# Splitting the second norm's operands group by group, with one head of ff1

## The chip, the cores and the metric

The kernel runs on one core of a Trainium2 chip. The metric is the device time of one execution in microseconds (us), as the median of several runs. The engines named here are TensorE (PE; its weight loads are shown as PEld), VectorE (DVE), ScalarE (ACT), GpSimd (POOL) and SyncE (SP); POOL and SP also issue DMAs, each in order from a queue of its own.

## The reference

One layer on 512 tokens of width 2048, all in float32:

```python
h = rmsnorm(x, g_mix)
z = h @ w_in                    # conv B, C, V | attention Q, K, V | forget logits | gates
conv_branch = (cb * causal_dwconv(cc * cv, conv_w)) @ w_conv_out
attn_branch = forgetting_attention(q, k, v, log_f) @ w_attn_out
merged = sigmoid(gate_c + ..) * conv_branch + sigmoid(gate_a + ..) * attn_branch
x = x + merged @ w_mix_out
h = rmsnorm(x, g_mlp)
u = square(relu(h @ w_ff1))     # 2048 -> 8192
x = x + u @ w_ff2               # 8192 -> 2048
out = rmsnorm(x, g_final)
```

## The kernel before

**Split operands.** Every matmul operand is split into a rounded high part and the rest: ACT copies it to a narrower float32 form (`th`, line 103), DVE subtracts that copy (`tl`, line 104). A product is then three matmuls: high by high, low by high, high by low. `th` and `tl` have two buffers each, so the next product's split runs beside the present one.

**Seven products for eight.** A `Group` (line 178) makes 512 columns of a product from four quarters X(i, j) of the weights, in Winograd's form: seven block products A11, A12, S1, S2, S3, S4, A22 of 48 matmuls each, instead of eight. DVE makes the sums of weight quarters (line 107) and puts the results together (line 110). The activations need the same seven combinations ("parts"), made and split beforehand. `head` runs A11 and A12, `tail`, `tail2` and `tail3` the other five in different orders; `head(True)` keeps its two quarters for the tail, `head()` lets them go, and the tail loads them again.

**Order of the stages.** Tile, the layer below, reorders instructions by its own estimate of when each is ready, engine by engine; what it leaves stands in order on each engine and queue. The stages that concern us follow one another so:

- `conv_out(c)` and `attn_out(c)`, c = 0 to 3: the two branches' projections, 512 columns each. `conv_out` multiplies its result by the convolution gate and, for c > 0, stores it in `held_d`; `bring(c)` loads it back into `merged`; `attn_out` adds the gated attention branch to it. `all_of(c)` makes and splits the seven parts of `merged[c]` into tiles `M` (placed by `M.place` in the buffers t0 to t6).
- Mixing groups g = 0 to 3 (`Mix`, line 1010): the product with `w_mix_out` and the residual sum. `turn` transposes each result with PE into `F`; `sums` makes the parts of the second norm's output from it. For g < 3 they are stored unsplit in `f_d` (`out`, line 1066).
- While group 3 and the first heads of ff1 run, `begin_part` loads each part from `f_d` into one of t0 to t6, and `split_part` splits it; group 3's own quarter is split straight into place.
- ff1: groups 0 to 15. Five `heads` of groups 0 to 4 run early, with `tail2` later; groups 5 to 15 run as head and `tail`. `put_u` squares the results, makes their parts for ff2 and stores them in `s_d`; `r` and `rh` have one buffer each. For the five early groups the squared first quarter goes through DRAM (`hu_d`).
- ff2: eight segments of two units each; `load_sums` loads the parts of a segment into t1 to t4.

**Starts.** The tiles `th` and `tl` are a little longer than their contents: a group of 256 columns starts `shift` elements into the tile. Groups have `SHIFT = 16` elements (64 bytes), mixing group g has `16 * g`: 0, 64, 128 and 192 bytes. In the mixing and value groups (`mm_rows`) this tile streams; in the others (`mm_cols`) it is the stationary operand. Some products start with one short extra matmul of 192 columns (`extra="first"`, `apart`), which changes no result.

Of the kernel before, what the change touches and what calls it, by code (L numbers as in the profile page):

```python
# [8 lines left out]
F32 = mybir.dt.float32  # L9
# [3 lines left out]
ALU = mybir.AluOpType  # L13
# [32 lines left out]
def tile_hybrid_block(ctx: ExitStack, tc, x, g_mix, w_in, b_f, b_gate, conv_w, w_conv_out,  # L46
# [33 lines left out]
    f_d = dram.tile([P, 7, KT // 2 - 2, HS], F32, name="f_d")  # L80
    hu_d = dram.tile([5, P, 2, HS], F32, name="hu_d")
# [20 lines left out]
    def split(src, hi, lo, one=1.0):  # L102
        nc.scalar.activation(out=hi, in_=src, func=AF.Copy, scale=one)  # L103
        nc.vector.tensor_tensor(out=lo, in0=src, in1=hi.bitcast(F32), op=ALU.subtract)  # L104

    def sub(out, a, b):
        nc.vector.tensor_tensor(out=out, in0=a, in1=b, op=ALU.subtract)  # L107
# [70 lines left out]
    class Group:  # L178
# [3 lines left out]
        def __init__(self, view, c1, c2, w, ST, mm, banks, put, scale=1.0, extra={}, after={}, shift=SHIFT):  # L182
            self.extra, self.after, self.shift = extra, after, shift
            self.view, self.cs, self.w, self.ST, self.mm, self.banks = view, (c1, c2), w, ST, mm, banks
            self.put, self.scale, self.at = put, scale, {}
            self.nq = view.shape[0] // (2 * P)
# [103 lines left out]

        def tail2(self):
# [3 lines left out]
            sub(X[0, 0], X[0, 1], X[0, 0])  # L295
            c = self.acc("c")
            self.run(c, "S1", X[0, 0], True)
            sub(X[0, 1], X[1, 1], X[0, 1])
# [553 lines left out]
    class Products:  # L852
# [5 lines left out]
        def tile(self, t, units):  # L858
            for e, u in enumerate(units):
                self.at[u] = t[:, e]  # L860
# [4 lines left out]
        def moving(self, n):  # L865
            return lambda q: tuple(self.at[n, q // 2][:, e, q % 2, :] for e in range(2))

        def quads(self, c, t):
# [3 lines left out]
            def put(n, src):  # L872
                split(src, self.at[n, c][:, 0], self.at[n, c][:, 1])
# [27 lines left out]
    def conv_out(c, banks):  # L901

        gates = {}
        for i, j in ((0, 0), (1, 1), (0, 1), (1, 0)):
            gates[i, j] = pc_.tile([P, 2, HS], F32, tag="hg", name="gates", bufs=4)
            k = 4 * c + 2 * j
            nc.gpsimd.dma_start(out=gates[i, j], in_=g_d[0, k:k + 2, :, i * HS:(i + 1) * HS].rearrange("k p s -> p k s"))
        if c == 0:
            place_merged(c)
# [22 lines left out]
    def place_merged(c):  # L932

        if c < 3:
# [36 lines left out]
    M.place(4, [(n, 0) for n in ("A11", "A12", "S1", "S3")])  # L971
    M.place(6, [("S2", 0), ("S4", 0), ("A22", 0), ("A22", 1)])
# [7 lines left out]
    M.place(1, [("S1", 1), ("S3", 1), ("S1", 2), ("S3", 2)])  # L980
    M.place(5, [("S2", 1), ("S4", 1), ("S2", 2), ("S4", 2)])
# [3 lines left out]
    M.tile(pm.tile([P, 1, 2, 2, HS], F32R, tag="m22", name="M"), [("A22", 2)])  # L985
# [13 lines left out]
    PARTS = ("A11", "A12", "A22", "S1", "S3", "S2", "S4")  # L999

    def begin_part(n, k):

        Q2[n] = pair(k, F32R, n).rearrange("p e (q s) -> p e q s", q=KT // 2)
        nc.gpsimd.dma_start(out=Q2[n][:, 1, :KT // 2 - 2].bitcast(F32), in_=f_d[:, PARTS.index(n)])

    def split_part(n):
        lo = Q2[n][:, 1, :KT // 2 - 2]
        split(lo.bitcast(F32), Q2[n][:, 0, :KT // 2 - 2], lo)

    class Mix:  # L1010


        def __init__(self, g):
            self.g, self.last = g, g == 3
            self.F = [pm.tile([P, 2, 2, HS], F32, tag=f"f{i}", name="f") for i in range(2)]
            self.x, self.missing = {}, []
# [19 lines left out]
        def turn(self, i, j, v):  # L1036
# [7 lines left out]
            if self.last and i == 0:  # L1044
                for par, n in enumerate(("A11", "A12")):
                    if n not in Q2:
                        self.missing.append((n, par, j))
                        continue
# [426 lines left out]
```

## Time and profile before

| | |
|---|---|
| Median of 3 runs | 2476.23 us (2475.4 to 2479.29) |
| Profiled execution, its own time | 2482.86 us |
| Its span | 2481.2 us, granted PE clock 0.991 |
| PE / weight load / DVE / ACT / POOL busy | 98% / 92% / 82% / 48% / 11% |
| HBM read, written | 385.47 MB, 107.48 MB |

The profile is one execution with every instruction's start and end. A row `L104 DVE TENSOR_TENSOR tl<-x,th ... x280 | 639.6, 2288 | 168.8` names line, engine, operation, what it writes and reads, how often, its total busy us, the mean ns of one, and the engine's idle time before these. In the order of time a row begins with start and duration in us; a bracket gives the idle time before it and what ended it. `A`, `S` and `M` are parts of activations, `x` and `y` weight quarters.

### The profile page before, as it was taken

To read this page: it belongs to the slowest core of one execution; us is meant where nothing else is said; L and a number is where in the kernel's file an instruction comes from. 1 tells how busy PE (TensorE), PEld (TensorE's weight loads), DVE (VectorE), ACT (ScalarE), POOL (GpSimd) and SP (SyncE) were. 2 spreads that over 40 slices of the span, in tenths; PEclk is the share of its full clock that TensorE was granted. 3 is DMA by queue.
4 is the path that set the end of the run, shared out by engine and by line. 5 is a ranking of instruction groups with operands and counts; after the bars stand their busy time and mean duration, and the time that the engine had idled before them with its cause. 6 is when DMAs were issued, how large, how long until landed. Compare 5 with 4: busy or idle time off the path is not lost. (4 is left out here: it accounts for less than half of the span.)

```text
span 2481.2 us, 41527 instructions
## 1 busy us (share of the span) xinstructions
PE 2425.0 (98%) x17799; PEld 2280.6 (92%) x17799; DVE 2044.8 (82%) x1711; ACT 1201.6 (48%) x1223; POOL 277.7 (11%) x443
## 2 busy tenths in 40 slices
PE   8999999999999999999898999999999999999998
PEld 8999899999999999899898899999997888888886
DVE  6987777688888778788887788988988888889898
ACT  6433443445545534355655556666665333333334
POOL 0100000111111111112100000000011000100000
PEclk9999999999999999999999999999999999999999
DMA  7564544464555755565856656466587566655763
GB/s 247 181 193 145 158 131 130 136 191 152 196 196 180 255 186 197 166 197 186 277 195 231 234 190 239 174 211 224 188 286 269 203 240 213 244 183 185 257 217 105
DMA packets 295788, 495.64 MB, mean 200 GB/s; under 512 B 11932, under 2 KB 208660, under 8 KB 295220
## 3 DMA queue, kind: packets, MB, share of 16 engines
q1 hardware_dynamic: 246432, 292.64, 37.3%
q0 software_dynamic: 48304, 199.25, 21.7%
q8 instruction: 139, 2.28, 0.4%
q10 hardware_dynamic: 868, 1.10, 0.1%
q14 instruction: 45, 0.37, 0.0%
HBM read 385.47 MB, written 107.48 MB: 199 GB/s over the span
## 5 line engine op out<-in xcount | busy, mean ns | idle before, releaser
L104 DVE TENSOR_TENSOR tl<-x,th 128x2048 fp32r<-128x2048 f32 (+1 forms) x280 | 639.6, 2288 | 168.8 <-ACT th L103 153.6
L103 ACT ACTIVATE th<-x 128x2048 fp32r<-128x2048 f32 (+1 forms) x280 | 536.6, 1917 | 476.2 <-DVE x L107 135.3
L107 DVE TENSOR_TENSOR x<-x,x 128x2048 f32<-128x2048 f32 (+1 forms) x160 | 366.1, 2288 | 32.5 <-DMA x<-in_w_in_dram 16.0
L103 ACT ACTIVATE th<-y 128x2048 fp32r<-128x2048 f32 (+1 forms) x109 | 184.8, 1700 | 270.3 <-PE a L167 138.9
L104 DVE TENSOR_TENSOR tl<-y,th 128x2048 fp32r<-128x2048 f32 (+1 forms) x109 | 219.0, 2014 | 25.7 <-ACT th L103 25.2
L147 PE MATMUL c<-S,th 128*128 128x256 f32 x912 | 212.1, 278 | 2.8 <-ACT o L212 2.8
L149 PE MATMUL c<-S,th 128*128 128x256 f32 x912 | 211.4, 277 | 0.0
L166 PE MATMUL a<-th,us 128*128 128x512 f32 x512 | 199.9, 390 | 2.0 <-ACT th L103 2.0
L167 PE MATMUL a<-th,us 128*128 128x512 f32 x512 | 200.0, 391 | 0.0
L147 PE MATMUL a<-S,th 128*128 128x256 f32 x720 | 169.6, 280 | 5.4 <-ACT th L103 5.4
L147 PEld LDWEIGHTS c<-S,th 128*128 128x128 f32 x912 | 171.4, 188 | 3.7 <-ACT o L212 3.2
L149 PEld LDWEIGHTS c<-S,th 128*128 128x128 f32 x912 | 171.4, 188 | 0.0
L149 PE MATMUL a<-S,th 128*128 128x256 f32 x720 | 168.0, 278 | 0.0
L147 PEld LDWEIGHTS a<-S,th 128*128 128x128 f32 x720 | 136.4, 189 | 6.0 <-ACT th L103 6.0
L147 PE MATMUL b<-A,th 128*128 128x256 f32 x544 | 130.2, 283 | 8.7 <-ACT th L103 8.7
L169 PE MATMUL a<-tl,us 128*128 128x512 f32 x512 | 137.3, 390 | 0.0
L149 PEld LDWEIGHTS a<-S,th 128*128 128x128 f32 x720 | 136.5, 190 | 0.0
L149 PE MATMUL b<-A,th 128*128 128x256 f32 x544 | 129.7, 282 | 0.0
L147 PE MATMUL a<-A,th 128*128 128x256 f32 x544 | 126.7, 278 | 0.0
L147 PE MATMUL d<-S,th 128*128 128x256 f32 x544 | 126.6, 278 | 0.0
L149 PE MATMUL a<-A,th 128*128 128x256 f32 x544 | 126.5, 278 | 0.0
L149 PE MATMUL d<-S,th 128*128 128x256 f32 x544 | 126.0, 277 | 0.0
(367 smaller groups left out, 6088.2 us busy)
## 6 DMA issues: line engine op xcount, KB each, us to landing
x<-in_w_in_dram SPq DMA_DIRECT2D x86, 1024.0 KB, 5.9
x<-in_w_ff_dram SPq DMA_DIRECT2D x74, 1024.0 KB, 8.0
y<-in_w_ff_dram SPq DMA_DIRECT2D x64, 1024.0 KB, 7.8
us<-s_d POOLq DMA_DIRECT2D x48, 1024.0 KB, 9.4
s_d<-rh POOLq DMA_DIRECT2D x32, 896.0 KB, 5.3
s_d<-r POOLq DMA_DIRECT2D x32, 896.0 KB, 8.2
x<-in_w_mix_out_dram SPq DMA_DIRECT2D x16, 1024.0 KB, 6.5
g_d<-o POOLq DMA_DIRECT2D x32, 256.0 KB, 2.8
```

Of the source, the lines that this page charges most:

```text
L103: nc.scalar.activation(out=hi, in_=src, func=AF.Copy, scale=one)
L104: nc.vector.tensor_tensor(out=lo, in0=src, in1=hi.bitcast(F32), op=ALU.subtract)
L107: nc.vector.tensor_tensor(out=out, in0=a, in1=b, op=ALU.subtract)
L147: nc.tensor.matmul(o, hi[:, q, js], Sh, start=first and q == 0 and j == 0, stop=False, skip_group_check=True)
L149: nc.tensor.matmul(o, hi[:, q, js], Sl, start=False, stop=False, skip_group_check=True)
L166: nc.tensor.matmul(o, Sh, hi[:, q, :], start=begin and q == 0, stop=False, skip_group_check=True)
L167: nc.tensor.matmul(o, Sl, hi[:, q, :], start=False, stop=False, skip_group_check=True)
L169: nc.tensor.matmul(o, Sh, lo[:, q, :], start=False, stop=q == nq - 1, skip_group_check=True)
```

## The change

- Each mixing group g < 3 splits its parts S1, S2, S3, S4 and A22 when it makes them, in a pair of `staged` buffers, and stores both halves in `h_d`. A11 and A12 still go unsplit to `f_d` and are split after loading. The five parts are handed out over the next group's products (`give`) instead of all at once.
- `begin_part` of the last group loads whole split parts; two parts come before ff1, more as buffers come free.
- ff1 has one head ahead: group 0 runs `head(True)` and `tail2`, groups 1 to 15 run like 5 to 15 before. `hu_d` and `fetch` go.
- `conv_out(1)`, `(2)` and `(3)` follow one another; the convolution gate of c > 0 is multiplied in `attn_out` from a tile `hg` of its own, and `bring` runs two column groups ahead.
- `M` holds parts by product rather than by column group, so that buffers come free product by product; the third A22 waits in `staged` and is copied.
- Some steps are kept in program order: behind the instruction traced before them on their engine.
- All mixing groups start at `shift=48` (192 bytes).
- Two of the first `load_sums` of ff2 are issued after A12 of the first unit.

The core of the diff:

```diff
-    f_d = dram.tile([P, 7, KT // 2 - 2, HS], F32, name="f_d")
-    hu_d = dram.tile([5, P, 2, HS], F32, name="hu_d")
+    f_d = dram.tile([P, 2, KT // 2 - 2, HS], F32, name="f_d")
+    h_d = dram.tile([P, 5, 2, KT // 2 - 2, HS], F32, name="h_d")
...
+    def split_in_order(*how):
+        for i in split(*how):
+            tc.keep_in_program_order(i)
...
+        def first_sum(self):
+            self.pinned = True
+            X = self.X
+            X[0, 1] = self.load(0, 1)
+            tc.keep_in_program_order(sub(X[0, 0], X[0, 1], X[0, 0]))
...
-            sub(X[0, 1], X[1, 1], X[0, 1])
+            third = sub(X[0, 1], X[1, 1], X[0, 1])
+            if self.pinned:
+                tc.keep_in_program_order(third)
...
     def conv_out(c, banks):
...
         def put(i, j, v):
             ts = slice(i * HS, (i + 1) * HS)
-            o = whole_of[c][:, i, :, j, :] if c == 0 else v
-            nc.vector.tensor_tensor(out=o, in0=v, in1=gates[i, j], op=ALU.mult)
-            if c > 0:
-                nc.gpsimd.dma_start(out=held_d[c, 2 * j:2 * j + 2, :, ts].rearrange("k p s -> p k s"), in_=o)
+            if c == 0:
+                nc.vector.tensor_tensor(out=whole_of[c][:, i, :, j, :], in0=v, in1=gates[i, j], op=ALU.mult)
+            else:
+                nc.gpsimd.dma_start(out=held_d[c, 2 * j:2 * j + 2, :, ts].rearrange("k p s -> p k s"), in_=v)
...
         def cons_at(j, ps):
+            if c > 0:
+                hg = otile([P, S], "hg")
+                nc.gpsimd.dma_start(out=hg, in_=g_d[0, 4 * c + j])
+                onto(c, j, hg, ALU.mult)
...
             if last and j == 2:
-                M.place(2, [(n, 3) for n in ("A11", "A12", "S1", "S3")])
-                M.place(3, [(n, 3) for n in ("S2", "S4", "A22")])
+                M.place(2, [(n, 3) for n in ("A11", "A12", "S1", "S2")])
+                M.place(3, [("S4", 3), ("S3", 3), ("A22", 3), ("A22", 2)])
+                for e in range(2):
+                    nc.gpsimd.dma_start(out=M.at["A22", 2][e].bitcast(F32), in_=m22[e].bitcast(F32))
...
     def all_of(c):
         for step in M.quads(c, merged[c]).values():
             step()
-        bring(c + 1)
+        if c < 2:
+            bring(c + 2)
...
     conv_out(0, lower)
     attn_out(0, upper)
     conv_out(1, lower)
-    attn_out(1, upper, between={0: lambda: all_of(0)})
-    conv_out(2, lower)
-    conv_out(3, upper)
-    M.place(0, [("A11", 1), ("A12", 1), ("A11", 2), ("A12", 2)])
...
+    conv_out(2, upper)
+    conv_out(3, lower)
+    M.place(0, [("A11", 0), ("A11", 1), ("A11", 2), ("A12", 0)])
...
+    m22 = M.at["A22", 2] = staged(), staged()
+    bring(1)
+    attn_out(1, upper, between={0: lambda: all_of(0)})
     attn_out(2, lower, between={0: lambda: all_of(1)})
     attn_out(3, upper, between={0: lambda: all_of(2)}, order=(0, 2, 1, 3), last=True)
...
     def begin_part(n, k):
         Q2[n] = pair(k, F32R, n).rearrange("p e (q s) -> p e q s", q=KT // 2)
-        nc.gpsimd.dma_start(out=Q2[n][:, 1, :KT // 2 - 2].bitcast(F32), in_=f_d[:, PARTS.index(n)])
+        if n in SPLIT:
+            nc.gpsimd.dma_start(out=Q2[n][:, :, :KT // 2 - 2].bitcast(F32), in_=h_d[:, SPLIT.index(n)])
+        else:
+            nc.gpsimd.dma_start(out=Q2[n][:, 1, :KT // 2 - 2].bitcast(F32), in_=f_d[:, int(n == "A12")])
...
             else:
-                nc.gpsimd.dma_start(out=f_d[:, PARTS.index(n), 2 * g:2 * g + 2], in_=src)
+                hi = staged()
+                split_in_order(src, hi, src)
+                for e, o in enumerate((hi.bitcast(F32), src)):
+                    nc.gpsimd.dma_start(out=h_d[:, SPLIT.index(n), e, 2 * g:2 * g + 2], in_=o)
...
             after.add("A11", before.sums)
+            for n, part in (("A12", "S1"), ("S1", "S3"), ("S2", "A22")):
+                after.add(n, lambda before=before, part=part: before.give(part))
...
             after.add("A12", lambda: begin_part("A11", 0))
-            after.add("S1", lambda: split_part("A11"))
-            after.add("S4", mix.fourth)
-            after.add("S3", lambda: begin_part("A12", 4), lambda: split_part("A12"), mix.supply)
-            after.add("A22", lambda: begin_part("S1", 1))
+            after.add("S2", lambda: begin_part("S1", 1), lambda: begin_part("S3", 2))
+            after.add("S4", mix.fourth, lambda: split_part("A11"))
+            after.add("S3", lambda: begin_part("S2", 5))
+            after.add("A22", lambda: begin_part("S4", 6), lambda: begin_part("A22", 3), lambda: split_part("A12"))
         group = Group(w_mix_out, g * S, g * S + HS, HS, M.moving, mm_rows, steady(g), mix.put, after=after,
-                      shift=16 * g)
+                      shift=48)
+        if g == 0:
+            after.add("A11", group.first_sum)
...
-    heads = [ff1(g, ((a,), (3,), (1,), (7,))) for g, a in enumerate((5, 0, 2, 4, 5))]
...
-    heads[3].tail2()
-    heads[4].tail2()
+    g0 = ff1(0, ((5,), (0,), (1,), (7,)))
+    g0.after = Steps(A11=[turn_waiting, mix.sums], A12=[lambda: mix.out("S1", mix.parts["S1"]),
+                                                        lambda: factors(common, turned)])
+    g0.head(True)
+    for n in SPLIT[1:]:
+        mix.out(n, mix.parts[n])
...
+    g0.tail2()
...
-    for g in range(AHEAD, DFF // S):
+    for g in range(1, DFF // S):
...
-    load_sums(0, (1, 2, 3), us0)
+    load_sums(0, (1,), us0)
...
+        if seg == 0 and cg == 0:
+            load_sums(0, (2, 3), us0)
```

More of the change, by code (lines that the diff above doesn't have):

```diff
@@ L865, in moving @@
         def moving(self, n):
[L866 removed]
+            return lambda q: tuple(e[:, q % 2, :] for e in self.at[n, q // 2])
         def quads(self, c, t):
@@ L1055, in turn @@
             if (i, j) == (0, 1) and not self.last:
-                for par, n in enumerate(("A11", "A12")):
-                    self.out(n, self.F[0][:, par])
-        def supply(self):
-            for n, par, j in self.missing:
-                split(self.F[0][:, par, j], *(Q2[n][:, e, 2 * self.g + j, :] for e in range(2)))
+                for par in range(2):
+                    nc.gpsimd.dma_start(out=f_d[:, par, 2 * g:2 * g + 2], in_=self.F[0][:, par])
         def fourth(self):
@@ L1079, in sums, with give @@
             sub(a12, a12, a11)
-            self.parts = {"S1": s1, "S3": a21, "S2": a11, "S4": a12, "A22": a22}
+            self.parts = {"S2": a11, "S4": a12, "S1": s1, "S3": a21, "A22": a22}
             if not self.last:
-                for n, src in self.parts.items():
-                    self.out(n, src)
+                self.give("S2", "S4")
+        def give(self, *names):
+            for n in names:
+                self.out(n, self.parts[n])
     waiting = []
@@ L1186, in put @@
             quarters[i, j] = v
-            if (i, j) == (0, 0) and g < AHEAD:
-                square(v, v)
-                nc.gpsimd.dma_start(out=hu_d[g], in_=v)
-            elif (i, j) == (0, 0):
+            if (i, j) == (0, 0):
                 later.append(hold)
```

80 lines of the change are left out of this document (28 added, 52 removed).

## The prediction, as made before the run

> **What bounds the kernel now.** I read the page first, then busy time by stretches, then the waits and the order of time inside the stretches that fell short. The page says that TensorE (PE) is the bound, and that at most 56 us of its span are idle (2481.2 less 2425.0):
>
> ```profile
> span 2481.2 us, 41527 instructions
> ...
> PE 2425.0 (98%) x17799; PEld 2280.6 (92%) x17799; DVE 2044.8 (82%) x1711; ACT 1201.6 (48%) x1223; POOL 277.7 (11%) x443
> ```
>
> A busy share hides slow matmuls, so I count matmuls per stretch. The columns are PE, weight load, DVE, ACT and POOL busy with counts, granted clock, DMA share, GB/s. In order: the last convolution group, mixing groups 0 to 3, the first head of ff1, its other heads, its tails, one steady ff1 group.
>
> ```profile
> 968.00:989.50 21.50, 20.34 (x172) 19.67 (x172) 18.97 (x23) 11.01 (x14) 4.37 (x6) 1.00 0.58 196
> 1033.60:1081.60 48.00, 44.15 (x344) 43.45 (x343) 40.09 (x40) 23.16 (x29) 3.63 (x5) 0.93 0.40 116
> 1081.60:1123.00 41.40, 41.40 (x354) 41.33 (x353) 32.86 (x25) 21.82 (x36) 9.71 (x15) 1.00 0.64 198
> 1123.00:1165.00 42.00, 41.89 (x356) 41.69 (x354) 33.36 (x25) 22.08 (x36) 9.69 (x15) 1.00 0.61 194
> 1165.00:1215.00 50.00, 43.21 (x355) 42.80 (x353) 39.65 (x33) 29.84 (x50) 13.15 (x21) 0.90 0.80 265
> 1215.00:1250.00 35.00, 35.00 (x302) 35.00 (x301) 31.59 (x30) 25.17 (x30) 5.49 (x8) 1.00 0.71 230
> 1250.00:1317.00 67.00, 65.83 (x579) 65.64 (x578) 53.83 (x37) 35.65 (x36) 3.80 (x7) 1.00 0.66 219
> 1317.00:1453.70 136.70, 119.75 (x963) 117.74 (x964) 109.40 (x86) 72.59 (x77) 9.66 (x18) 0.95 0.63 213
> 1492.00:1530.10 38.10, 38.10 (x338) 38.10 (x337) 33.76 (x27) 24.40 (x26) 2.13 (x4) 1.00 0.59 208
> ```
>
> The steady row gives 38.10/338 = 0.1127 us per matmul. Each stretch less its count at that pace is what it loses: 2.1, 9.2, 1.5, 1.9, 10.0, 1.0, 1.7 and 28.2 us. The start of ff2, with matmuls twice as wide, is set against its next 27 us (27/121 each):
>
> ```profile
> 1857.00:1884.00 27.00, 24.96 (x106) 19.92 (x105) 23.70 (x19) 15.87 (x17) 2.61 (x4) 0.94 0.85 304
> 1884.00:1911.00 27.00, 27.00 (x121) 22.37 (x120) 24.31 (x14) 13.60 (x12) 3.05 (x5) 1.00 0.69 252
> ```
>
> It loses 3.3. All stretches that the diff touches thus lose about 59 us; more than that the change cannot gain.
>
> **ff1 with one head.** Five heads run before any tail, and a head that does not keep its two quarters loads them again. The waits between 1317 and 1453.7 say what this costs (waiter, releaser, total us, times, longest):
>
> ```profile
> PE b L147 <- ACT th L103: 8.7, 2, 4.6
> ACT r L1154 <- DMA s_d<-r: 12.8, 2, 7.0
> ACT r L1149 <- DMA s_d<-r: 10.7, 2, 5.4
> DVE x L107 <- DMA x<-in_w_ff_dram: 4.8, 2, 3.5
> ```
>
> PE waits for ACT's copy `th`; ACT stands in order behind work on `r`, whose single buffer is still being stored; DVE waits for weights. In the DMA issues one sees the reload and the square's round trip:
>
> ```profile
> x<-in_w_ff_dram SPq DMA_DIRECT2D x74, 1024.0 KB, 8.0
> hu_d<-o POOLq DMA_DIRECT2D x5, 256.0 KB, 2.5
> f_d<-f POOLq DMA_DIRECT2D x18, 256.0 KB, 3.5
> S<-f_d POOLq DMA_DIRECT2D x4, 768.0 KB, 6.4
> ```
>
> Sixteen groups of four quarters are 64 loads; 74 means ten repeats, 10 MB. After the change groups 1 to 15 run the code that groups 5 to 15 run now, and that code loses nothing in the steady row. So 28.2 + 1.7 = **-29.9**; the least is about -20 if a third of it comes from being near the norm rather than from the heads.
>
> **The start of ff1.** Removed are the splits of S1, S3, S2, S4 and A22 read back raw; only their last quarter is split there. What remains hangs on the last mixing product: its sum on DVE, transposes, sums, split of S1. First and last step in order of time, and between them what DVE did of splits in that stretch:
>
> ```profile
> 1215.29 0.69 DVE L110 TENSOR_TENSOR o<-d,o 128x512 f32<-128x512 f32 x1 [2.12 <-PE d L169]
> L104 DVE TENSOR_TENSOR S<-S 128x1536 fp32r<-128x1536 f32 x2 | 3.5, 1755 | 0.3 <-ACT S L103 0.3
> L104 DVE TENSOR_TENSOR A<-A 128x1536 fp32r<-128x1536 f32 x1 | 1.8, 1753 | 0.0
> 1230.79 0.67 DVE L104 TENSOR_TENSOR S<-s,S 128x512 fp32r<-128x512 f32 x1
> ```
>
> Today the chain takes 1231.46 - 1215.29 = 16.2 us with three splits of 1.75 in it, and three heads cover it. One head covers 96 matmuls, 10.8 us. The three splits go and A12's comes in (-3.5), and a subtraction for S1's weights (2.28, a row below) must fit in: 15.0 on a DVE that is not always free, but part of it overlaps with ACT. Bounds: 0, if DVE takes the chain first, and 10 (16.2 + 2.3 + 1.9 for `th`, less 10.8). I take **+4**.
>
> **Mixing group 3.** The order of time shows one blocked copy:
>
> ```profile
> 1194.15 0.57 POOL L1004 DMA_DIRECT2D S<-f_d  x1 [10.51 <-PE c L169]
> 1201.96 1.48 ACT L103 ACTIVATE S<-S 128x1536 fp32r<-128x1536 f32 x1 [6.30 <-DMA S<-f_d]
> PE d L166 <- ACT th L103: 6.8, 1, 6.8
> ```
>
> ACT waits 6.3 us for a part that POOL asked for at 1194; the `th` of A22 stands behind it, and PE stops. The clock row 0.90 is the echo: slow matmuls after the stop. In the new kernel S1 to A22 need no copy after loading; A11 and A12 do, but A11 is loaded after A12 and split three products later, and the pin keeps it behind the copy traced before. Of 10.0 I take **-8.5**; at least -3 if A12's split, now at the end of the group, holds ACT likewise.
>
> **Start at 192 bytes.** Ten microseconds inside groups 0, 1, 2, 3 (starts of 0, 64, 128, 192 bytes), in an ff1 tail and in a steady ff1 group (both 64):
>
> ```profile
> 1070.00:1080.00 10.00, 10.00 (x86) 1.00 0.87 253
> 1106.00:1116.00 10.00, 10.00 (x88) 1.00 0.75 209
> 1148.00:1158.00 10.00, 10.00 (x87) 1.00 0.72 208
> 1189.00:1199.00 10.00, 10.00 (x90) 1.00 0.97 317
> 1339.00:1349.00 10.00, 10.00 (x87) 1.00 0.98 307
> 1500.00:1510.00 10.00, 10.00 (x91) 1.00 1.02 368
> ```
>
> Only 192 keeps nearly the steady pace. But the last two rows have one start and two paces, so the start alone does not set it; it seems to go with whether a stop came before. If it does hold, 4/90, 2/90 and 3/90 of some 40 us each are saved: **-4.0**; bounds 0 and -5.2 (1.5 + 1.9 + 1.8).
> By the Trainium skill's page "SBUF — State Buffer", section "Specifications (TRN2)", what counts for reads is the 16-byte line; all four starts are multiples of 16, so by that rule alone this term would be 0 and the sum four higher. The rows 86 to 90 side with a difference.
>
> **Into the mixing.** Group 0 loses 9.2, of which 1.8 is pace. DVE runs two weight subtractions ahead of the last merge:
>
> ```profile
> 1032.46 2.28 DVE L107 TENSOR_TENSOR x<-x,x 128x2048 f32<-128x2048 f32 x1
> 1035.93 2.28 DVE L107 TENSOR_TENSOR x<-x,x 128x2048 f32<-128x2048 f32 x1
> 1038.63 0.63 ACT L103 ACTIVATE M<-merged 128x512 fp32r<-128x512 f32 x1 [3.12 <-DVE merged L930]
> ```
>
> The pin on the third sum moves the later one behind the merge. The earlier one may stay; its pin sets it only behind A11's split. Bringing the held quarters in two column groups ahead also lets DVE start on them earlier. Of 7.4: **-6**, bounds 0 and -7.4.
>
> **Convolutions in a row.** The gate product leaves three convolution groups (4 products of 128x512, 0.69 of DVE each by the next row but one) for the attention groups. With it go twelve of the gate loads:
>
> ```profile
> gates<-g_d POOLq DMA_DIRECT2D x16, 256.0 KB, 4.2
> ```
>
> As many loads as before stand on POOL, now beside the held quarters and in the buffers that the other gates use. Where POOL waits for such a buffer, the held quarters behind it come later; they are needed only when the last weight chunk of their attention group is through, so I cost that at nothing, and at one landing (4.2) if that cover is gone, inside the range. The one convolution group that follows another today loses 2.1, and two will follow one, each with 2.8 less of DVE. I take **0**, bounds -2.1 and +2.1. The copy of A22's third operand out of `staged`, two more stores on POOL, is wanted six products later: nothing.
>
> **New splits in groups 1 to 3.** Five copies and five subtractions of 128x512 per group, and ten stores on POOL where five were.
>
> ```profile
> L104 DVE TENSOR_TENSOR M<-merged,M 128x512 fp32r<-128x512 f32 x24 | 16.4, 687 | 1.6 <-ACT M L103 1.4
> ```
>
> DVE in group 2 goes from 33.4 to 36.8 us, against 356 x 0.1127 = 40.1 of PE: 92%, where the steady ff1 group runs at 89% without loss. I take **+2**; bounds 0 and 10 (fifteen subtractions of 0.69, none covered). Behind a pinned copy stand ACT's `th` copies, for which PE waits. The reads back on POOL wait for the product that frees their buffer; S4 and A22, asked for when group 3 is over, are first used five products later (27 us), against 6.4 us for today's half as large loads: nothing.
>
> **Start of ff2.** Two of three loads of sums are traced after A12. They are still free to go when their buffers are: **-1**, bounds -3.3 and +1.
>
> **Sum:** -29.9 + 4 - 8.5 - 4.0 - 6 + 0 + 2 - 1 = -43.4. The profiled execution took 2482.86 (span 2481.2 and 1.7 around it), 6.6 above the median 2476.23 of the three timed ones. From its own time the sum gives 2439.5; from the median **2432.8**, which I forecast as 2433.
>
> **Rivals.**
> *Slower: the pinned copies hold ACT.* Fifteen copies into two `staged` buffers may each wait until a store has landed. A store of this size takes 3.5 (row above); with none covered, 15 x 3.5 = 52 on PE, 2485. It ends slower once a hold costs PE 43.4/15 = 2.9 on the mean. For it: the blocked copy at 1201.96 is this mechanism. Against: ACT is idle 19.9 of 42 us in group 2, and pairs of parts are mostly a product apart. Chance 0.09.
> [...]
> *Loads collide at the norm.* Five parts of 1.5 MB, twice today's, come within some 45 us beside weights. Group 3 already has DMA at 0.80 and 265 GB/s, so weights may come as late as in the tails: three waits of 4 (8.7 in two times, above), 2445. Chance 0.10.
> *The pins do not do what they say.* They order a step behind one other only. If both hoists return elsewhere, 8.5 + 6 come back: 2447. Chance 0.10.
> *The start does nothing:* 2437. Chance 0.05.
>
> **Numbers.** The forecast has 0.63; these rivals 0.34; 0.03 stays for no change. Faster by over 0.2% (5 us, about what a measurement of this kernel can tell from no change) 0.88, within 0.03, slower 0.09. All best ends give 2418, all worst 2476 - 20 + 10 - 3 + 2 + 10 + 1 = 2476. Neither set of ends is likely to meet; the range is 2419 to 2463, which holds three rivals and leaves the slower one out.
>
> **What would show it.** Right: 64 loads of ff1 weights; each ff1 group from 1 on at 38.2 us with no PE wait; no gap of 7 us before A22; 90 matmuls in 10 us in every mixing group. Wrong: PE waits for `th` in groups 1 to 3 with ACT behind a store; a gap before S1 of ff1's first group above 10 us.

## The result, and the profile after

The changed kernel takes 2458.48 us (median of four runs, 2455.73 to 2464.36), the kernel before 2477.76 beside it. The ratio is 0.9924, with a 95% interval of 0.9899 to 0.9949. It is faster, by 19 us where 43 were forecast; the time lies inside the forecast's range (2419 to 2463), near its slow end. A second set of six runs gave 2458.94 and 0.9928 (0.9913 to 0.9942).

The page of the profiled execution (2464.36 us, one of the longer ones) gives the engines' busy times and the DMA issues. In the changed kernel the sums stand at other lines: subtractions of weights and parts at L113, additions at L116.

```profile
span 2462.6 us, 41554 instructions
...
PE 2408.8 (98%) x17800; PEld 2264.8 (92%) x17800; DVE 2041.8 (83%) x1729; ACT 1201.8 (49%) x1233; POOL 279.8 (11%) x450
...
x<-in_w_ff_dram SPq DMA_DIRECT2D x64, 1024.0 KB, 8.3
```

The 74 loads of ff1 weights are 64. PE is busy for 16 us less, and still idle for 54. The same columns as in the prediction's table by stretch, here cut where a stage's first matmul stands. In order: the three convolution groups, the three attention groups, the first two products of the mixing, the rest of its group 0, groups 1, 2 and 3, the first two products of ff1 (with the last of the mixing between them), the rest of ff1, ff2.

```profile
905.28:966.95 61.67, 59.19 (x511) 58.23 (x510) 47.83 (x51) 30.81 (x37) 7.84 (x12) 1.00 0.41 130
966.95:1032.98 66.03, 65.84 (x290) 53.91 (x289) 52.38 (x77) 21.19 (x23) 17.86 (x28) 1.00 0.80 269
1032.98:1057.90 24.92, 16.04 (x97) 15.04 (x96) 14.74 (x21) 6.62 (x7) 0.71 (x1) 0.73 0.20 65
1057.90:1090.09 32.19, 29.13 (x251) 28.30 (x249) 26.59 (x22) 16.29 (x22) 2.91 (x4) 1.00 0.55 164
1090.09:1131.35 41.26, 40.66 (x355) 40.44 (x354) 34.85 (x29) 24.41 (x41) 12.34 (x20) 1.00 0.71 226
1131.35:1175.57 44.22, 41.91 (x355) 41.72 (x354) 36.04 (x29) 24.52 (x41) 12.34 (x20) 0.96 0.66 215
1175.57:1214.57 39.00, 34.89 (x308) 34.52 (x306) 37.26 (x33) 26.70 (x42) 13.41 (x22) 1.00 0.72 240
1214.57:1238.90 24.33, 19.73 (x158) 19.49 (x157) 17.03 (x18) 11.82 (x26) 6.48 (x8) 0.93 1.02 393
1238.90:1839.22 600.32, 600.32 (x5300) 600.32 (x5298) 523.65 (x395) 373.87 (x376) 37.55 (x67) 1.00 0.60 210
1839.22:2462.62 623.40, 610.86 (x2690) 503.83 (x2688) 537.11 (x400) 242.98 (x175) 55.85 (x75) 0.99 0.61 213
```

The kernel before, cut at the same places where the prediction cut elsewhere (its convolution group 1; the other convolution and attention groups; the start of the mixing; the rest of group 0; ff1 from S1 of its first group on, which here stands behind three heads; ff2):

```profile
907.33:926.61 19.28, 19.28 (x171) 19.28 (x170) 16.87 (x21) 11.67 (x14) 2.91 (x4) 1.00 0.32 105
926.61:1033.58 106.97, 105.80 (x630) 92.92 (x629) 84.13 (x97) 39.67 (x45) 21.02 (x29) 1.00 0.67 220
1033.58:1052.06 18.48, 14.63 (x98) 13.92 (x96) 15.64 (x21) 7.42 (x8) 0.72 (x1) 0.82 0.05 16
1052.06:1081.64 29.58, 29.58 (x251) 29.58 (x249) 24.50 (x20) 15.78 (x22) 2.91 (x4) 1.00 0.62 179
1249.93:1857.53 607.60, 589.48 (x5107) 587.28 (x5105) 514.11 (x383) 361.83 (x364) 40.46 (x73) 0.99 0.62 216
1857.53:2481.16 623.63, 612.16 (x2690) 505.21 (x2688) 537.30 (x400) 242.95 (x175) 56.02 (x75) 0.99 0.61 213
```

What a stage loses is again its length less its matmuls at 0.1127 us. ff1 lost 607.60 - 5107 x 0.1127 = 32.0 and loses 3.0: the large term came. But the first two products of the mixing lose 24.92 - 97 x 0.1127 = 14.0 where they lost 7.4, and the rest of group 0 loses 3.9 where it lost 1.3. The waits between 1020 and 1070 us, and rows of POOL and VectorE in order of time, show the first of these (`hg` is the convolution gate that the attention groups now load, `gt` the attention gate):

```profile
PE a L172 <- ACT M L103: 5.7, 1, 5.7
DVE merged L948 <- DMA hg<-g_d: 3.7, 1, 3.7
```

```profile
1029.42 0.54 POOL L971 DMA_DIRECT2D hg<-g_d  x1 [1.93 <-DVE merged L948]
...
1040.00 0.42 DVE L948 TENSOR_TENSOR merged<-merged,hg 128x256 f32<-128x256 f32 x1 [3.72 <-DMA hg<-g_d]
...
1061.12 2.29 DVE L113 TENSOR_TENSOR x<-x,x 128x2048 f32<-128x2048 f32 x1
```

POOL could ask for the last gate `hg` only at 1029.42, after a merge had freed its buffer; DVE waits for it until 1040.00. It was asked for late, and it also landed slowly: these some 10 us stand against a median of 4.6 for the twelve gate loads. PE stops for 5.7 us, and then its matmuls are slow for a while: the clock column reads 0.73 for the whole stretch. At 1061.12 stands the weight subtraction that the second pin, the one on the third sum, has moved there.

At the norm (1200 to 1245 us), waits and then two steps of VectorE in order of time:

```profile
DVE x L113 <- DMA x<-in_w_ff_dram: 7.1, 2, 4.5
PE ptr L1075 <- DVE o L116: 6.9, 2, 4.6
```

```profile
1228.22 2.29 DVE L113 TENSOR_TENSOR x<-x,x 128x2048 f32<-128x2048 f32 x1 [2.57 <-DMA x<-in_w_ff_dram]
1230.43 0.68 DVE L116 TENSOR_TENSOR o<-o,xr 128x512 f32<-128x512 f32 x1
```

PE's transposes wait for the sum `o`, for 4.6 us at 1231.17. The sum could be made, but it stands on DVE behind two subtractions of ff1 weights that landed late: DVE waits 4.49 us for the first and 2.57 for the second. In that stretch DMA is busy throughout (1.02, 393 GB/s). The other stop of PE there, 2.3 us at 1214.18, is for sums that stand on DVE behind the split of A12 (1.75 us, at 1210.96).

### The profile page after: what moved, and what is told of

Read it like the earlier page. It is cut to its first block, busy times and chain, and to the rows that moved or that the text cites. A ratio compares the mean times of both kernels' runs of the same rounds, so it can differ in the third digit from the quotient of the medians.

```text
span 2462.6 us, 41554 instructions
## 1 busy us (share of the span) xinstructions
PE 2408.8 (98%) x17800; PEld 2264.8 (92%) x17800; DVE 2041.8 (83%) x1729; ACT 1201.8 (49%) x1233; POOL 279.8 (11%) x450
## 4 chain that ended last, share of the span: by engine, by line
PE 48%; DVE 4%; DMA 3%; issue 2%; ACT 1%; POOL 0%; DVEq 0%; POOLq 0%; ACTq 0%
PE a L175 5%; PE a L173 5%; PE a L172 5%; PE a L153 3%; PE a L155 3%; PE a L157 3%; PE d L175 2%; PE d L153 2%; PE d L155 2%; PE d L172 2%; PE d L173 2%; PE d L157 2%; DVE tl L104 2%; PE c L153 1%; PE c L155 1%
## 5 line engine op out<-in xcount | busy, mean ns | idle before, releaser
L113 DVE TENSOR_TENSOR x<-x,x 128x2048 f32<-128x2048 f32 (+1 forms) x160 | 365.9, 2287 | 29.8 <-DMA x<-in_w_in_dram 16.0
L104 DVE TENSOR_TENSOR tl<-y,th 128x2048 fp32r<-128x2048 f32 (+1 forms) x109 | 219.0, 2013 | 26.0 <-ACT th L103 25.5
L153 PE MATMUL c<-S,th 128*128 128x256 f32 x848 | 196.5, 277 | 0.0
L155 PE MATMUL c<-S,th 128*128 128x256 f32 x848 | 196.0, 277 | 0.0
L153 PE MATMUL a<-S,th 128*128 128x256 f32 x784 | 182.2, 278 | 0.0
L155 PE MATMUL a<-S,th 128*128 128x256 f32 x784 | 180.8, 276 | 0.0
L153 PEld LDWEIGHTS c<-S,th 128*128 128x128 f32 x848 | 159.3, 188 | 0.3
L155 PEld LDWEIGHTS c<-S,th 128*128 128x128 f32 x848 | 159.3, 188 | 0.0
L155 PEld LDWEIGHTS a<-S,th 128*128 128x128 f32 x784 | 147.3, 188 | 0.0
L153 PEld LDWEIGHTS a<-S,th 128*128 128x128 f32 x784 | 147.2, 188 | 0.0
L153 PE MATMUL b<-A,th 128*128 128x256 f32 x544 | 127.2, 278 | 0.0
L155 PE MATMUL b<-A,th 128*128 128x256 f32 x544 | 127.1, 278 | 0.0
```

The costliest lines, as they stand in the source:

```text
L104: b = nc.vector.tensor_tensor(out=lo, in0=src, in1=hi.bitcast(F32), op=ALU.subtract)
L113: return nc.vector.tensor_tensor(out=out, in0=a, in1=b, op=ALU.subtract)
L153: nc.tensor.matmul(o, hi[:, q, js], Sh, start=first and q == 0 and j == 0, stop=False, skip_group_check=True)
L155: nc.tensor.matmul(o, hi[:, q, js], Sl, start=False, stop=False, skip_group_check=True)
```

## The experiments

Two questions were open: what stops the start of the mixing (the gates' loads, or the order on VectorE), and whether the bytes of the split parts or the work on them delays the norm. All ratios are against the kernel before; the changed kernel has 0.9928 (0.9913 to 0.9942).

**Gates in other buffers.**

```
-                hg = otile([P, S], "hg")
+                hg = pm.tile([P, S], F32, tag=("xr", "s1")[j % 2], name="hg")
```

> The attention gates of column groups 1 to 3 (hg) get two buffers of their own, those of xr and s1, which stand idle until the mixing begins; nothing else changes. Theory A (the gates take the shared o buffers, so their loads and those of gt are issued late and land late): the stop at the start of the mixing, where TensorE waits 5.7 us for the copy M and VectorE 3.7 us for hg, shrinks to under 2 us, the stalls behind it go with it, and the time falls by 6 to 11 us from 2458.5. Rival B (VectorE is late there because the pinned weight subtraction of 2.28 us and the merges stand in one line): the wait for hg goes, TensorE still waits 4 us or more, and the time changes by less than 3 us.

2460.71 us, ratio 0.9923 (0.9903 to 0.9943): no gain. The attention groups, the start of the mixing, and the waits from 990 to 1033 us:

```profile
966.94:1043.02 76.08, 68.34 (x291) 54.82 (x290) 54.58 (x79) 21.41 (x23) 18.53 (x29) 0.98 0.76 248
1043.02:1060.60 17.58, 13.89 (x98) 13.09 (x97) 12.27 (x19) 6.62 (x7) 0.71 (x1) 0.90 0.07 21
```

```profile
PE pt L401 <- DVE tl L104: 5.8, 3, 2.3
DVE merged L948 <- DMA hg<-g_d: 5.7, 2, 4.7
```

The start is 7.3 us shorter, and PE's wait for the copy `M` there falls from 5.7 us to 0.8, as theory A had it; but the attention groups are 10.0 longer. With two buffers a gate is asked for only when the one two before it has been used, so DVE waits for it earlier, and the split of attention weights `tl` that PE needs stands behind that wait. Theory A had the start right and the time wrong; rival B had the time right (within 3 us), but not the stop, which it said would stay. The run shows that it is when the gate loads can start that counts, and that two buffers are fewer than they need.

**Gates back in the convolution groups.** The loads of `gates` (four buffers) and the product are again made in every `conv_out`, and `attn_out` has no `hg`.

> The gate product of column groups 1 to 3 goes back to the convolution groups, with its own four buffers there, as in the kernel before; the order of the groups and all else stays. Theory A: as with own buffers, the start of the mixing loses at most the 7.4 us of the kernel before instead of 14, so 6 to 11 us come back, less up to 2 us for VectorE's 0.69 us products in the three convolution groups. Rival B: the stop stays within 1 us of its 5.7 us, and the time is within 3 us of 2458.5 or slower.

2454.26 us, 0.9891 (0.9869 to 0.9912). The three convolution groups, the start of the mixing, the rest of group 0:

```profile
908.07:971.05 62.98, 59.91 (x511) 58.88 (x510) 54.03 (x61) 30.75 (x37) 13.09 (x18) 1.00 0.50 166
1036.61:1049.60 12.99, 11.52 (x98) 11.12 (x96) 8.82 (x10) 6.40 (x7) 0.00 (x0) 1.00 0.07 22
1049.60:1081.81 32.21, 29.20 (x251) 28.37 (x249) 26.67 (x22) 16.31 (x22) 2.91 (x4) 1.00 0.55 164
```

Theory A holds: the start takes 12.99 in place of 24.92, and the clock column reads 1.00. The convolution groups give 1.3 us back. By medians the whole gains 4.7 of these 10.6, by the two ratios some 9, and their intervals hold both; group 3 took 2.9 us more in this profile (41.93, against 39.00). The rest of group 0 has not moved: its loss has another cause.

**No kept order in group 0.**

```
-            tc.keep_in_program_order(sub(X[0, 0], X[0, 1], X[0, 0]))
+            sub(X[0, 0], X[0, 1], X[0, 0])
...
-            if self.pinned:
-                tc.keep_in_program_order(third)
```

> The two weight subtractions of group 0 are not kept in program order; all else stays. Theory E (the pinned third sum puts 2.28 us of VectorE in front of the copy that S3 of group 0 waits for): the stretch from S1 of group 0 to its last product falls from 32.2 to 30 us or less, the start of the mixing, which waits for the gates, stays within 1 us, and 1 to 3 us come back. Rival (the pins earn what the prediction gave them): the start of the mixing grows by 2.3 to 4.6 us, one or two subtractions, and the kernel is that much slower.

2453.15 us, 0.9901 (0.9886 to 0.9917). The start of the mixing and the rest of group 0:

```profile
1032.99:1056.06 23.07, 15.36 (x97) 14.65 (x96) 17.12 (x23) 7.30 (x8) 0.71 (x1) 0.78 0.24 74
1056.06:1084.31 28.25, 28.25 (x251) 28.25 (x249) 24.02 (x20) 15.78 (x22) 2.91 (x4) 1.00 0.63 187
```

The rest of group 0 falls from 32.19 to 28.25 us, all of it busy at the steady pace: theory E, and 5.8 us by medians. The subtraction makes the weights that S3's copy reads. Pinned, it came at 1061.12, behind other work of a VectorE that had been busy since 1055.12, and PE waited 1.5 us for the copy; freed, it runs at 1041.67. The start did not grow. Which of the two pins it was can be read from the built program: with the third sum freed and the first still kept, every engine's order is that of this kernel, so the first pin does nothing. The traces agree: the first sum runs at 1032.72 with its pin and at 1032.81 without.

**The changed kernel once more.**

> The changed kernel once more, as it is, to see how far its stages differ from one execution to the next. Theory C (weight loads that come late among stores and reads of the parts): the stretches of groups 1 to 3 and of the norm, 148.8 us together in the first profile, differ by 4 us or more, since the times of single executions run from 2455.7 to 2464.4; theory A: the stretch from the first product of the mixing to S1 of its group 0 stays at 24.9 within 1 us. Rival: both repeat within 1 us, and the spread lies elsewhere.

2458.94 us; its profile has a span of 2456.0, against 2462.6 in the first. Groups 2 and 3 and the norm here:

```profile
1131.34:1173.25 41.91, 41.23 (x356) 40.83 (x353) 36.78 (x30) 24.71 (x41) 12.37 (x20) 1.00 0.70 229
1173.25:1210.87 37.62, 35.23 (x308) 35.05 (x306) 35.76 (x33) 26.55 (x42) 13.46 (x22) 0.99 0.76 253
1210.87:1229.88 19.01, 19.01 (x158) 19.01 (x156) 15.42 (x14) 10.72 (x23) 6.10 (x8) 0.93 1.01 387
```

They are 2.3, 1.4 and 5.3 us shorter than in the first profile, with the same program; the start of the mixing is 25.09, as before. The stops of PE behind late weights (in the first profile 2.3 us at the start of group 2, 1.8 at that of group 3 and 4.6 at the norm) are 0.6, none and none at these places here. So they come in some executions and not in others, and a single profile does not price them. The loss at the start of the mixing stands in both profiles, and so does the stop behind A12's split (2.3 and 2.4 us).

**Half the stores; half the reads; half of both.**

```
-                for e, o in enumerate((hi.bitcast(F32), src)):
-                    nc.gpsimd.dma_start(out=h_d[:, SPLIT.index(n), e, 2 * g:2 * g + 2], in_=o)
+                nc.gpsimd.dma_start(out=h_d[:, SPLIT.index(n), 1, 2 * g:2 * g + 2], in_=src)
...
-            nc.gpsimd.dma_start(out=Q2[n][:, :, :KT // 2 - 2].bitcast(F32), in_=h_d[:, SPLIT.index(n)])
+            nc.gpsimd.dma_start(out=Q2[n][:, 1, :KT // 2 - 2].bitcast(F32), in_=h_d[:, SPLIT.index(n), 1])
```

> Leaves out the stores of the high halves of the split parts (15 of 30 stores of 256 KB in groups 1 to 3); the reads move as many bytes as before, both from the low half, so the operands of ff1 are other numbers. The copies and subtractions stay. Theory C (the stores collide with the weight loads): the two waits of 2.3 and 1.8 us in which TensorE's transposes stand behind a late weight load in groups 1 and 2 go, the weight loads there take under 9 us instead of 12.9, and 4 to 9 us come back. Rival D (the copies and subtractions of the splits are what delays VectorE): the waits stay and the time is within 2 us of 2458.5.

> Reads back only the low half of each split part (0.75 MB in place of 1.5 MB, five times) and uses it for both operands in ff1, so ff1 computes with other numbers; stores, copies and subtractions stay. Theory C: the two waits of TensorE for the norm's transposes between 1203 and 1236 us, 6.9 us together, fall under 2 us, the ff1 weight loads there take under 11 us instead of 16.6 and 17.1, and 5 to 10 us come back. Rival D: they stay, since the same VectorE work stands before the transposes, and the time is within 2 us of 2458.5.

> Leaves out both the stores of the high halves and the reads of them: the low half serves for both operands of ff1, which so computes with other numbers. Copies, subtractions and their order stay. Theory C (the bytes of the parts, 3.75 MB more stored and read back than as one half each, make the weights late): the stretch from the start of group 1 to S1 of ff1's first group, 148.8 and 139.5 us in the two profiles of the changed kernel, comes to 138 or less, single executions lie within 4 us of each other, and 4 to 8 us come back. Rival D (VectorE's work and its order): the stretch stays at 139 or more and the time is within 2 us of 2458.9.

Half the stores: 2456.78 us, 0.9907 (0.9886 to 0.9928). Half the reads: 2458.06, 0.9910 (0.9891 to 0.9929). Each lies within the 2 us of 2458.5 that theory D allowed, and the stops that they lack are also lacking when the changed kernel is profiled again; neither decides. Both: 2453.14, 0.9896 (0.9879 to 0.9913), 5.8 us by medians, and all four runs lie below all ten of the changed kernel. The norm here:

```profile
1212.36:1230.99 18.63, 18.22 (x159) 17.98 (x157) 17.17 (x18) 12.24 (x26) 5.40 (x8) 1.00 0.87 316
```

DMA is no longer full (0.87), and the ff1 weights asked for from 1200 to 1232 us land sooner than in the first profile of the changed kernel (its row first; in its second profile two loads take 14.3):

```profile
x<-in_w_ff_dram SPq DMA_DIRECT2D x3, 1024.0 KB, 16.6
```

```profile
x<-in_w_ff_dram SPq DMA_DIRECT2D x3, 1024.0 KB, 9.9
```

From the start of group 1 to S1 of ff1's first group it takes 137.8 us, within theory C's 138, where the changed kernel took 148.8 and 139.5. Theory C is borne out at about 6 us for all of the extra bytes, but not in its second part: the single runs still lie 4.8 us apart. The run also leaves out 15 of the 30 stores as such, so it does not part the bytes from the number of transfers.

**The reads one product later.** `begin_part` of S1, S3 and S2 is moved behind S4, S3 and A22 of group 3.

> In group 3 the reads of the split parts S1 and S3 are asked for one product later, and that of S2 with those of S4 and A22 after the last product; all else stays. Theory C: the stores of the parts no longer stand behind the read of S1, the ff1 weights land sooner, the 6.9 us for which TensorE waits with the norm's transposes shrink to under 3, and 3 to 6 us come back. Rival G (the bytes set it, not their order): the waits move to S1 or S3 of ff1's first group, which then wait for their operand, and the time is within 2 us of 2458.5 or slower by up to 5.

2456.32 us, 0.9912 (0.9897 to 0.9927); the norm takes 19.66 us, against 24.33 and 19.01 in the two profiles of the changed kernel. The gain is 2.6 us by medians, the intervals overlap, and rival G is not excluded.

**The start of the weights.**

```
-                      shift=48)
+                      shift=16 * g)
```

> The weights of the four mixing groups start at 0, 64, 128 and 192 bytes as in the kernel before; all else stays. Theory F (the start sets the pace): the matmuls of groups 0, 1 and 2 go at 118 to 120 ns in place of 113, and 3 to 5 us are lost. Rival: the pace stays at 113 ns wherever no stop came before, and the time is within 1 us of 2458.5.

2458.17 us, 0.9919 (0.9903 to 0.9935): the same time. Ten microseconds inside group 1, and group 1 as a whole; first with a start of 64 bytes, then with 192 (the repeated run of the changed kernel):

```profile
1100.00:1110.00 10.00, 10.00 (x88) 10.00 (x87) 9.76 (x12) 4.64 (x9) 4.24 (x8) 1.00 0.36 132
1091.59:1133.01 41.42, 41.42 (x355) 41.34 (x353) 35.71 (x30) 24.25 (x41) 12.40 (x20) 1.00 0.71 227
```

```profile
1100.00:1110.00 10.00, 10.00 (x91) 10.00 (x90) 9.76 (x12) 4.40 (x8) 4.74 (x8) 1.00 0.39 135
1090.39:1131.34 40.95, 40.35 (x356) 40.16 (x354) 36.00 (x30) 24.51 (x41) 12.39 (x20) 1.00 0.72 227
```

Theory F had the pace right and the time wrong, its rival the other way round. The start does move the pace (88 matmuls in ten microseconds against 91). But in group 1 PE's busy time falls by 1.07 us, and 0.60 us of idle time appear that was not there: PE gets to its transposes sooner and waits for their sums from VectorE. Over the three stages whose start differs (the rest of group 0, groups 1 and 2) PE is busy for 113.84 us with the old starts and for 110.76 with 192 bytes, and the stages take 116.39 and 115.07: of 3.1 us saved, 1.3 are left. That is too little for the runs to tell. Nor does the start alone fix the pace: in group 2 of the second profile, at 192 bytes, one stretch of ten microseconds (1162 to 1172), all busy, holds 87.

**Both losses undone together**, then with the later reads as well.

> Both undone at once: the gate product goes back to the convolution groups, and the weight subtractions of group 0 are not kept in order. Theory A with E: both gains hold side by side, the stretch from the first product of the mixing to S1 of group 0 is at most 17 us in place of 25, the one from there to the end of group 0 at most 29 in place of 32.2, and the time is 2446 to 2450. Rival B: with the gates gone the subtraction that stands ahead of the last merge becomes what the start waits for, the first stretch is 18 us as in the kernel before, and the time is 2451 to 2455.

> As the one before, and in group 3 the reads of S1, S3 and S2 are asked for one product later. Theory C: with less in the queues when the ff1 weights are asked for, 1 to 4 us more come back, and the time is 2443 to 2448. Rival G: the time is that of the one before within 1.5 us.

2446.62 us, 0.9867 (0.9847 to 0.9887), and 2446.28, 0.9871 (0.9852 to 0.9891). This is 12 us less than the changed kernel and 32 less than the kernel before. Of the first of the two kernels the start of the mixing and the rest of group 0, and VectorE around that start:

```profile
1036.29:1047.93 11.64, 11.23 (x98) 11.02 (x97) 10.42 (x15) 7.27 (x8) 0.71 (x1) 1.00 0.08 25
1047.93:1076.73 28.80, 28.80 (x250) 28.64 (x249) 24.55 (x20) 15.82 (x22) 2.90 (x4) 1.00 0.64 183
```

```profile
1027.38 2.29 DVE L104 TENSOR_TENSOR tl<-x,th 128x2048 fp32r<-128x2048 f32 x1 [2.70 <-ACT th L103]
...
1033.66 2.28 DVE L113 TENSOR_TENSOR x<-x,x 128x2048 f32<-128x2048 f32 x1
```

The row of the kernel before that answers to the first of these:

```profile
1029.65 2.29 DVE L104 TENSOR_TENSOR tl<-x,th 128x2048 fp32r<-128x2048 f32 x1 [1.12 <-ACT th L103]
```

The start loses 0.6 us, although both subtractions run ahead of the last merges, as they did in the kernel before. Rival B falls here; with the pins kept (gates back) the start took 12.99. What differs from before is that DVE begins the first split of mixing weights 8.9 us ahead of the first product (1027.38 to 1036.29) and not 3.9 (1029.65 to 1033.58). In the attention groups of the kernel before (990 to 1033 us) DVE waited for a held quarter:

```profile
DVE merged L926 <- DMA merged<-held_d: 8.3, 1, 8.3
```

In this kernel, with the held quarters asked for two column groups ahead, no such wait is left between 990 and 1037 us. No run brings them ahead alone (the order of the convolution groups and the places of `M` changed with it), so this cause of the gain is likely and not shown. The later reads add nothing: rival G.

Group 3 takes 40.3 and 41.6 us in these two kernels, against 39.0 and 37.6 in the changed one. In the first of them PE waits twice in it:

```profile
PE ptr L1069 <- DVE o L116: 4.8, 2, 3.1
```

```profile
1160.88 2.29 DVE L113 TENSOR_TENSOR x<-x,x 128x2048 f32<-128x2048 f32 x1 [2.90 <-DMA x<-in_w_mix_out_dram]
...
1196.27 1.75 DVE L104 TENSOR_TENSOR A<-A 128x1536 fp32r<-128x1536 f32 x1
...
1199.26 0.68 DVE L116 TENSOR_TENSOR o<-d,o 128x512 f32<-128x512 f32 x1
```

The longer wait, 3.1 us, is at the start of the group (1163.83): the sums stand on VectorE behind a subtraction of mixing weights that landed late. At the end of the group (1199.49) PE waits 1.7 us for sums behind the kept split of A12. The expectation of the next run puts the 3.1 us at the end of the group, which misreads the trace.

**A12 split later.** On top of the two undone:

```
-            after.add("A22", lambda: begin_part("S4", 6), lambda: begin_part("A22", 3), lambda: split_part("A12"))
+            after.add("A22", lambda: begin_part("S4", 6), lambda: begin_part("A22", 3))
...
+    split_part("A12")
     g0.head(True)
```

> As the kernel with both losses undone, and the split of A12 is called behind the last sums of group 3, before ff1's first group, in place of inside the last product's step. Theory H (the kept split, 1.75 us on VectorE, stands ahead of the last three sums of group 3, for which the transposes of TensorE wait): the wait of 3.1 us at the end of group 3 shrinks by 1.5 to 3 us, the stretch of group 3, 40.3 there, comes to 37.5 to 38.8, and 1 to 3 us come back. Rival (the split is late wherever it stands): A12 of ff1, or the transposes behind it, wait for it instead, and group 3 with the first two products of ff1 take 59.9 within 1 us.

2450.67 us, 0.9888 (0.9869 to 0.9907): no gain, and some 4 us slower by medians, though the intervals overlap. The waits from 1190 to 1260 us:

```profile
DVE x L113 <- DMA x<-in_w_ff_dram: 7.8, 2, 6.2
PE ptr L1069 <- DVE o L116: 3.6, 1, 3.6
```

Neither expectation fits. The wait at the end of group 3 falls from 1.7 us to 0.3 (the stop for `o` shown here is a later one), and the 3.1 us at its start stay; but the next transposes now stand behind a late ff1 weight load. From the start of group 3 to ff2 it is 667.9 us, against 662.6. Perhaps the split was cover for a load that comes late in any case; since such loads differ from one execution to the next, one profile does not show it.

## Why the prediction was right and where it was wrong

The terms beside the stages of the two profiles of the changed kernel (against the one of before; the second stands nearer to the median). What a stage is said to gain is the change of what it loses:

| Term | Forecast | First | Second |
|---|---|---|---|
| ff1 with one head | -29.9 | -29.0 | -28.1 |
| Group 3 and start of ff1 | -8.5 + 4 | -0.2 | -6.9 |
| Into the mixing | -6 | +6.6 | +6.7 |
| Pace (-4.0) and new splits (+2), rest of group 0 to group 2 | -2 | +4.8 | +1.9 |
| Convolutions in a row | 0 | +1.5 | +1.4 |
| Start of ff2, here with all of ff2 | -1 | -0.2 | +1.3 |
| Before the convolutions (code not changed) | 0 | -2.0 | -1.9 |
| Sum | -43.4 | -18.5 | -25.5 |

The profiled execution of the kernel before is 5 us above its median, so the second profile gains more on it than the 19 us between the medians. Before the convolutions, where no code changed, the profiles of all kernels differ by 3 us (905.3 to 908.4). At the start of ff2 the term did not come: its first 27 us hold 103 matmuls in the kernel before, 104 and 100 in the changed one.

**Into the mixing** is the step that failed, by 12.7 us. Two statements behind it were wrong. The first is "I cost that at nothing", said of the twelve gate loads under "Convolutions in a row": they share the five `o` buffers with `gt`, two to each merge where one was, so the last of them is asked for at 1029.42 and is there some 10 us later, 3.7 us after VectorE is free for its merge. The prediction asked what comes later on POOL's queue, and not which merges on VectorE wait for the late gate itself. Its bound of one landing (4.2) was also too small, since the load took longer than that and the stop was followed by slow matmuls: of the 13.3 us between this stage in the changed kernel and in the one with both undone, 8.5 are idle time (24.92 - 16.04 less 11.64 - 11.23) and 4.8 are longer busy time. The second is that the pins were credited with the gain: the pin on the first sum does nothing, the pin on the third costs 3.9. The other reason given, the quarters brought ahead, is the likely one: with the gates and the pins out of the way the stage goes from 18.48 to 11.64, which is -6.8, and VectorE's wait of 8.3 us for a held quarter is gone. So the size of the term was right for a kernel without these two steps.

**New splits and pace.** The pinned third sum makes the +2.6 in the rest of group 0; without it the stage has no loss left. The pace came (91 against 88), most of the time did not: the prediction turned matmul counts into microseconds as though PE were the only bound there, with DVE at 88% of the stage (36.00 of 40.95). Of 3.1 us of busy time saved, 1.3 are left. Without the pin the rest of group 0 does keep its saving (29.58 before, 28.25). So -4.0 was mis-sized; the rival in which the start does nothing came nearer to this term's time, for the wrong reason.

**Group 3 and the start of ff1.** The 7 us before A22 went, as forecast. In their place are a shorter stop at the end of the group (2.3 and 2.4 us in the two profiles, behind the split of A12, which the prediction had named for ACT; it is VectorE that it holds), one at its start behind late mixing weights (1.8 us and none), and the rival of loads that collide at the norm (4.6 us and none). The last two are not fixed but come and go: the two stages are 4.3 us worse than forecast in the first profile and 2.4 better in the second. The rival was priced at 12 (2445 against 2433); all extra bytes together measured 6.

**ff1 with one head**, the largest term, was right within 2 us: 64 loads, and PE busy for all of the 600.32 us after group 0's start. The labels of two rows in the prediction's first table are wrong: the row from 1215 holds the first three heads (302 matmuls, 96 to a head), and the next holds the tails of groups 0 and 1 with the fourth head between them. So three heads, not five, run before any tail. The sum uses the losses of the rows and does not change with the labels.

**Convolutions in a row** stayed within its bounds. Weights come late there too: from 924 to 962 us VectorE waits 6.5 us, in two waits, for weights of the convolution's projection.

**The slower rival** did not happen. It decided from 2.9 us for each of fifteen copies; from 1057 to 1240 us ACT waited for a store with these copies twice (and once more, for 2.1 us, with a transposed result):

```profile
ACT staged L103 <- DMA h_d<-staged: 2.5, 2, 1.3
```

What stays open: with the two losses undone the kernel is still 13.6 above the forecast. The runs put some 6 of that on the bytes of the parts (measured on the changed kernel) and 1.3 on the product given back to the convolution groups; of the -4.0 of the pace some 1.3 was had. Group 3 takes 40.3 to 41.9 us in the kernels where the stages before it got shorter. Their profiles show where: 2.1 to 3.1 us at its start behind late mixing weights, and 1.7 to 4.0 at its end behind the split of A12. Which weight load comes late in which execution, and whether the shorter stages have a part in it, was not settled (half of the reads has 40.6 us without a shorter stage before).

## What to carry to other kernels

When an operand is fetched inside the step that uses it, count how many buffers its tag has for the loads of that whole step: a load that shares buffers with another starts when those come free, and everything behind its consumer on the same engine waits. Moving an instruction by a pin moves its whole duration to another place, so look at how full that engine is there. Where VectorE is nearly as busy as PE, price faster matmuls by what VectorE lets through: here, with VectorE busy for 83% to 88% of three stages, less than half of the 3.1 us that PE saved was left. Read a wait at its own place in the order of time before giving it a cause: the same waiter and releaser stood at both ends of group 3 here, with two causes.

## What the runs showed of the hardware

The start address of the weights that stream through a matmul changes the pace: with nothing else changed, group 1 of the mixing holds 88 matmuls in ten microseconds with a start at 64 bytes and 91 at 192, and PE is busy in it for 41.42 us (355 matmuls) and 40.35 (356). By the Trainium skill's page "SBUF — State Buffer", section "Specifications (TRN2)", a read pays for each cross to a new line of 16 bytes. Both starts are multiples of 16, and the runs show a difference that this rule does not have.

A stop costs more than its length: after 5.7 us without a matmul the clock column of the changed kernel reads 0.50 for the next 9.5 us (1041.52 to 1051.00, with two shorter stops in them), 0.63 from there to 1053.94 and 1.00 after that. The 97 matmuls of this stage took 16.04 us busy, against 11.23 for 98 in the kernel without the stop, where the column reads 1.00.
